# Up stages: the first pair's convolution, gating and block sums handed out in pieces between the products of the first two seven-product items

## The chip, the cores and the metric

The kernel runs on one core of a Trainium2 chip. The time is that of one execution in device microseconds (us). Four engines matter here: PE (TensorE, the matrix products), DVE (VectorE), ACT (ScalarE) and POOL (GpSimd); SP issues most of the transfers.

## The reference

A trunk of two layers on one sequence of S = 1024 rows, D = 1024 wide, in float32. Each layer has a mixer (layer 0 a gated delta rule, layer 1 retention) and a feed-forward part, each with a residual and a layer norm, scaled and shifted by vectors that come from a conditioning input through a product with an "adaptive" weight. The change touches the first half of the feed-forward part:

```python
def causal_dwconv(x, w):
    k_w = w.shape[0]
    s = x.shape[1]
    xp = jnp.pad(x, ((0, 0), (k_w - 1, 0), (0, 0)))
    y = xp[:, k_w - 1:k_w - 1 + s] * w[k_w - 1]
    for j in range(k_w - 1):
        y = y + xp[:, j:j + s] * w[j]
    return y

def conv_ffn(h, w_up, conv_w, conv_b, w_down):
    gate, up = jnp.split(h @ w_up, 2, axis=-1)
    gate = causal_dwconv(gate, conv_w) + conv_b
    return (jax.nn.silu(gate) * up) @ w_down
```

The hidden width is 2816, 22 tiles of 128, and the convolution has three taps along the sequence.

## The kernel before

**Numbers.** Every float32 operand of a product is split into a high part (an ACT copy, line 89) and a low part (a DVE subtraction, line 90); a product is three matmuls, lines 110 to 112 or, when it adds to a bank in use, line 1229. A matmul takes 128 x 128 weights and 512 columns.

**Up stage.** `layer_tail` runs the feed-forward part, once a layer. Its up product is cut into 22 items: 11 pairs of one gate item and one up item, each with 2 x 2 blocks (two tiles of the hidden width by two halves of the sequence). `strassen` runs them. The first two items (pair 0) are done plainly in four blocks: first the blocks that need the first half of the sequence (`side(n, 0)`, item 1 before item 0), whose results ACT copies out into `ahead` tiles (line 1256) because the second half of the normalized input is still being built (`build_T`, transposes at line 439, their copies at 441, sums over blocks at 464 to 470); then the rest (`side(n, 1)`). All items from 2 on go through `wino`, a Winograd scheme with seven products in place of eight. There `psub` (line 1279) makes sums of weight blocks on DVE, `block` splits each into a pair `wb`, and `prod` runs 12 matmuls on it.

**What a finished block does.** Each item has a sink, called with a result. A gate item's sink (line 1617 or 1619) puts it into `g`. After the fourth, `conv` does the three taps for the four blocks q = 0 to 3: ACT multiplies by the last tap (line 1628), DVE adds two taps (line 1633, two instructions a block), ACT applies the silu (line 1634). An up item's sink, `gated`, multiplies `o[q]` by the result (line 1647) and stores it; after the fourth, four sums and differences of the blocks (line 1654) make the operands of the down product's own seven-product scheme, and are stored too. In pair 0 these sums are on DVE, later on POOL.

**Order.** Each engine takes its instructions in one order, fixed when the program is built; a list scheduler sets it from the order of the code, so code that is written earlier tends to stand earlier. `bg_step` issues one unit of a background queue: products of the conditioning input with adaptive weights (`bg_ada`, lines 237 and 239 on DVE, for a row a matmul with ones at line 261 and an add at 262), and others. `wino` calls it twice an item. The first unit queued in an up stage is `bg_ada(i, 5, "row")`, the gain behind the feed-forward part. Layer 0's up stage is preceded by the output projection (`proj_ln`, lines 326 to 359) in two halves, with transposes for the first half (line 282) at the switch between them.

Of the kernel before, what the change touches and what calls it, by code (L numbers as in the profile page):

```python
# [12 lines left out]
ALU = mybir.AluOpType  # L13
# [20 lines left out]
def trunk_kernel(ctx: ExitStack, tc, A):  # L34
# [1188 lines left out]
    def strassen(hT0, xts, scale, shift, items, tags=("hTb", "hTb", "qkv", "qkv", "aux"), direct=False):  # L1223
# [23 lines left out]
        for n in (1, 0):  # L1247
# [6 lines left out]
            ahead[n] = [tl("cv", [P, 516], name="ah")[:, 0:HALF] for _ in range(2)]  # L1254
# [26 lines left out]

        def wino(n, sink):
            ua, ub = items[n][:2]
            wa, wb = tl("wr", [P, D]), tl("wr", [P, D])
# [15 lines left out]
            s4 = psub(a12, s2)  # L1300
            prod(s2, "T2", X)
            u2 = copy_of(X)
            s3 = psub(a11, a21)
            prod(s4, "22", Z)
            sink(1, Z, u2)
            bg_step()
            prod(s3, "T3", X)
            u3 = copy_of(X, "t2")
            sink(3, X, z5)
            sink(2, prod(a22, "T4"), u3)  # L1310
            bg_step()
# [4 lines left out]
        for n in range(2):  # L1316
            if not direct:
                sinks[n] = items[n][2]()
                for i in range(2):
                    sinks[n](2 * i, ahead[n][i], None)  # L1320
            X = side(n, 1)
            for i in range(2):
                sinks[n](2 * i + 1, X[i], None)
            if n == 0:
                rest()
            if items[n][3]:
                items[n][3]()
        for n in range(2, len(items)):
            wino(n, items[n][2]())
            if items[n][3]:  # L1330
# [252 lines left out]
    def layer_tail(i, mix, wout, xsrc, x_mid, x_out, ln_next, final):  # L1583
        sc2, sh2 = fold(i, 1, 2 * i)
        if i == 0:
            hT0 = []
# [6 lines left out]
            for h in hooks[KT:]:  # L1593
                h()
        else:
            mix.append((sc2, sh2))
            hT0, xts = proj_st(mix[0])
        bg_ada(i, 5, "row")
        bg_gain(2 * i, x_mid, xg[i + 1], "xT")
        if i == 0:  # L1600
            for j in (1, 0, 4, 3):
                bg_ada(1, j, "col")
        cw = vcol(f"ffn_conv{i}")
# [3 lines left out]

        def pair_items(fp):
            g, o = [], []
# [11 lines left out]

            def conv():
                for q in range(4):
                    f, hf = 2 * fp + q // 2, q % 2
                    gv = g[q // 2]
                    w = cw[:, 3 * f:3 * f + 3]
                    t = tl("qkv", [P, HALF], name="o")
                    act.activation(t, gv[:, hs(hf)], AF.Copy, scale=w[:, 2:3])  # L1628
                    for j in (1, 2):
                        c0 = HALF if hf else j  # L1630
                        c1 = HALF * (hf + 1)
                        tv = t[:, c0 - HALF * hf:]
# [390 lines left out]
```

## Time and profile before

| | |
|---|---|
| runs shown | 2936.68, 2944.91, 2948.51 us; median 2944.91 |
| the profiled execution | 2944.47 us, its span 2942.7 us |
| PE busy in the span | 2815.8 us, 13594 matmuls |
| DVE busy | 2208.4 us, 3976 instructions |
| ACT busy | 1314.9 us, 2413 instructions |
| POOL busy | 497.8 us, 517 instructions |
| mean granted TensorE clock | 0.983 |
| layer 0: last plain matmul of pair 0, first matmul of item 2 | 805.57, 810.65 us |
| layer 1: the same two | 2328.62, 2333.70 us |

Busy times overlap, since the engines run side by side. The span is from the first to the last instruction in the trace, and the execution's time has 1.77 us more around it. A time in a row of the trace counts from the span's start. In brackets behind a row stands how long the engine was idle before it, and which instruction ended that.

### The profile page before, as it was taken

Reading aid. Unit: us, or ns where it says so; the run is one execution under the profiler, and the core shown is the slowest. Engines: PE = TensorE matmul, PEld = TensorE weight load, DVE = VectorE, ACT = ScalarE, POOL = GpSimd, SP = SyncE. Lnnn points to the kernel's source line nnn. Section 1 sums busy time; section 2 is a strip of 40 time slices with the busy share of each in tenths; the row PEclk is TensorE's granted clock in tenths of the full one; section 3 lists DMA queues with packets and bytes.
Section 4 is the critical chain, followed back from the end, with each engine's and each line's share of the span. In section 5 each row is a group of like instructions: output and inputs, shape, how many; then the busy total and the mean of one; then the engine's idle time right before and its main releaser. Section 6 shows DMA issues by size and latency. Waiting matters only on the chain. (4 is left out here: it accounts for less than half of the span.)

```text
span 2942.7 us, 38900 instructions
## 1 busy us (share of the span) xinstructions
PE 2815.8 (96%) x13594; PEld 2298.3 (78%) x13594; DVE 2208.4 (75%) x3976; ACT 1314.9 (45%) x2413; POOL 497.8 (17%) x517
## 2 busy tenths in 40 slices
PE   8999899999999999999999999999999899999997
PEld 6887777887778888887778877777777788888886
DVE  6878788656688888868686665566689787777779
ACT  4745564444544444545333333222344544444543
POOL 0312221100013332200000021422202023331001
PEclk9999899999999999999999999999999999999999
DMA  7231222243255655755333364655663253334753
GB/s 279 80 119 62 80 79 80 83 167 137 93 176 175 208 189 188 270 185 184 132 136 115 129 231 145 208 171 170 194 231 131 102 165 133 135 126 162 291 184 115
DMA packets 248276, 459.01 MB, mean 156 GB/s; under 512 B 23632, under 2 KB 77264, under 8 KB 248080
## 3 DMA queue, kind: packets, MB, share of 16 engines
q1 hardware_dynamic: 215680, 404.87, 40.9%
q10 hardware_dynamic: 29760, 43.00, 4.0%
q0 software_dynamic: 2640, 8.65, 0.8%
q8 instruction: 107, 1.75, 0.2%
q14 instruction: 89, 0.73, 0.1%
HBM read 343.71 MB, written 112.72 MB: 155 GB/s over the span
## 5 line engine op out<-in xcount | busy, mean ns | idle before, releaser
L714 PE MATMUL acc<-hT,wh 128*128 128x512 f32 x960 | 301.3, 395 | 0.0
L1504 PE MATMUL acc<-bb,ab 128*128 128x512 f32 x984 | 236.2, 398 | 10.9 <-DVE bb L90 9.3
L1504 PEld LDWEIGHTS acc<-bb,ab 128*128 128x128 f32 x984 | 186.0, 191 | 55.2 <-DVE bb L90 14.2
L714 PEld LDWEIGHTS acc<-hT,wh 128*128 128x128 f32 x960 | 183.4, 191 | 34.5
L1229 PE MATMUL acc<-T,wb 128*128 128x512 f32 x840 | 203.6, 391 | 6.9 <-DVE wb L90 6.8
L89 ACT ACTIVATE ab<-ar 128x512 fp32r<-128x512 f32 x210 | 130.2, 626 | 171.2 <-PE mm L303 46.9
L714 PE MATMUL acc<-hT,wl 128*128 128x512 f32 x480 | 202.3, 421 | 0.0
L411 POOL TENSOR_TENSOR xg<-xg,gb 128x512 f32<-128x512 f32 x48 | 62.4, 1302 | 773.6 <-DMA xg<-xs 761.4
L1229 PEld LDWEIGHTS acc<-T,wb 128*128 128x128 f32 x840 | 156.5, 188 | 45.0 <-DVE wb L90 10.4
L90 DVE TENSOR_TENSOR ab<-ar,ab 128x512 fp32r<-128x512 f32 x210 | 147.5, 708 | 57.6 <-ACT ab L89 57.6
L90 DVE TENSOR_TENSOR wl<-wr,wh 128x1024 fp32r<-128x1024 f32 x98 | 123.0, 1256 | 86.9 <-ACT wh L89 86.7
L1654 POOL TENSOR_TENSOR o<-o 128x512 f32<-128x512 f32 x80 | 124.7, 1568 | 288.8 <-ACT pc L1290 190.1
L90 DVE TENSOR_TENSOR wb<-wr,wb 128x512 fp32r<-128x512 f32 x162 | 116.9, 726 | 71.6 <-ACT wb L89 69.4
L89 ACT ACTIVATE wh<-wr 128x1024 fp32r<-128x1024 f32 x98 | 103.9, 1062 | 143.5 <-PE acc L714 70.5
L90 DVE TENSOR_TENSOR wb<-mm,wb 128x512 fp32r<-128x512 f32 x216 | 145.8, 683 | 27.5 <-ACT wb L89 26.8
L1633 DVE SCALAR_TENSOR_TENSOR o<-g,vc,o 128x512 f32<-128x512 f32 (+2 forms) x176 | 155.0, 897 | 5.3 <-ACT o L1628 4.6
L89 ACT ACTIVATE wb<-mm 128x512 fp32r<-128x512 f32 x216 | 124.0, 595 | 64.4 <-DVE mm L1279 61.3
L1290 ACT ACTIVATE pc<-acc 128x512 f32<-128x512 f32 x143 | 84.6, 592 | 144.2 <-PE acc L1229 88.5
L89 ACT ACTIVATE wb<-wr 128x512 fp32r<-128x512 f32 x162 | 98.6, 627 | 107.6 <-DMA wr<-in_ffn_up 50.2
L714 PE MATMUL acc<-wh,hT 128*128 128x512 f32 x384 | 135.2, 416 | 1.0 <-DVE vv L90 1.0
L110 PE MATMUL acc<-T,wb 128*128 128x512 f32 x292 | 116.0, 397 | 9.4 <-DVE wb L90 9.4
L490 DVE SCALAR_TENSOR_TENSOR qkv<-raw,vc,qkv 128x512 f32<-128x512 f32 x144 | 110.3, 769 | 14.2 <-ACT qkv L488 13.5
(651 smaller groups left out, 7456.4 us busy)
## 6 DMA issues: line engine op xcount, KB each, us to landing
wr<-in_ffn_up SPq DMA_DIRECT2D x92, 512.0 KB, 4.3
mvw<-in_ada_w SPq DMA_DIRECT2D x80, 512.0 KB, 4.4
ad<-o SPq DMA_DIRECT2D x154, 256.0 KB, 3.1
ar<-ad SPq DMA_DIRECT2D x154, 256.0 KB, 3.8
Br<-in_ffn_down SPq DMA_DIRECT2D x88, 256.0 KB, 3.4
wr<-in_ret_wv SPq DMA_DIRECT2D x32, 512.0 KB, 4.2
ar<-od SPq DMA_DIRECT2D x56, 256.0 KB, 4.9
wr<-in_gdn_wqkv SPq DMA_DIRECT2D x24, 512.0 KB, 3.5
```

The costliest lines, as they stand in the source:

```text
L89: act.activation(dst_h, src, AF.Copy)
L90: eng.tensor_tensor(dst_l, src, dst_h, ALU.subtract)
L110: mm(acc, wl[:, k], hl[0], start=first, stop=False)
L411: pool.tensor_tensor(x, x, gb[0], ALU.mult)
L490: dve.scalar_tensor_tensor(oh, raw[:, 3 - j:515 - j], w[:, 3 - j:4 - j], oh, ALU.mult, ALU.add)
L714: pq(pe.matmul(out, lhsT, rhs, start=start, stop=stop), cost)
L1229: return pe.matmul(*a, skip_group_check=True, **kw)
L1290: act.activation(t, X, AF.Copy)
L1504: return pe.matmul(*args, skip_group_check=True, **kw)
L1633: dve.scalar_tensor_tensor(tv, gv[:, c0 - j:c1 - j], w[:, 2 - j:3 - j], tv, ALU.mult, ALU.add)
L1654: (dve if fp == 0 else pool).tensor_tensor(o[d], o[x], o[y], op)
```

## The change

Only `strassen` and `layer_tail` are touched, and of `strassen` only the calls from the two up stages take the new paths.

- A list `late` holds pieces of work. `drain(n)` takes up to n of them off its front and issues them. `wino` drains two behind s4's difference, two behind s3's, two behind the sink of block 1 and two behind the sink of block 3; behind every item from 3 on, all that is left.
- Pair 0's convolution goes into the list as four pieces, in the order q = 1, 3, 0, 2, where it ran at once for q = 0 to 3. Then come the gating of the two blocks just computed, the gating of the two `ahead` blocks, and the four block sums, one piece each. A gating piece first issues pieces until its own block's convolution has been issued. Pair 1's convolution goes through the list too.
- While the list holds work at an item's start, that item calls no `bg_step`. Layer 0's `bg_ada(0, 5, "row")` is queued ahead of the output projection, with its weights in "xT" tiles; layer 1's stays in the up stage, behind the gain.
- The two `ahead` copies of item 1 share one "xT" tile in place of two "cv" tiles.

The number of instructions on each engine is the same before and after; POOL's order is unchanged.

DVE at the entry of item 2 in layer 0, up to the low half of the first block `wb`, which the first product waits for. `T4` is the last low half of the input's sums, `o` the convolution's blocks and `g` a gate result of item 2; the scalar multiply-and-add of the convolution is printed as TENSOR_SCALAR. Before:

```order
L90 TENSOR_TENSOR T4_7372<-bt_7213,T4_7371 128x512
L1633 TENSOR_SCALAR o_7375<-g_7223,vc_144,o_7375 128x511
L1619 TENSOR_TENSOR g_7472<-sc_7501,pc_7494 128x512
L1633 TENSOR_SCALAR o_7380<-g_7223,vc_144,o_7380 128x512
L1633 TENSOR_SCALAR o_7375<-g_7223,vc_144,o_7375 128x510
L1633 TENSOR_SCALAR o_7385<-g_7224,vc_144,o_7385 128x511
L1633 TENSOR_SCALAR o_7390<-g_7224,vc_144,o_7390 128x512
L1633 TENSOR_SCALAR o_7380<-g_7223,vc_144,o_7380 128x512
L90 TENSOR_TENSOR wb_7517<-mm_7496,wb_7517 128x512
```

After, from the same low half of `T4`:

```order
L90 TENSOR_TENSOR T4_7415<-bt_7256,T4_7414 128x512
L1661 TENSOR_SCALAR o_7545<-g_7266,vc_144,o_7545 128x512
L1648 TENSOR_TENSOR g_7480<-sc_7509,pc_7502 128x512
L1661 TENSOR_SCALAR o_7550<-g_7267,vc_144,o_7550 128x512
L1661 TENSOR_SCALAR o_7545<-g_7266,vc_144,o_7545 128x512
L90 TENSOR_TENSOR wb_7525<-mm_7504,wb_7525 128x512
```

Of the eight convolution steps six stood between `T4` and `wb`, and three do now.

The next stretch of DVE there, up to the low half of the second product's block. `ada` is the adaptive row, `mm` a sum of weight blocks, `ah` and `acc` the up results that gate `o`. Before:

```order
L237 TENSOR_SCALAR ada_7609<-mvw_7572,e_154 128x512
L1633 TENSOR_SCALAR o_7385<-g_7224,vc_144,o_7385 128x510
L1647 TENSOR_TENSOR o_7375<-o_7375,ah_7071 128x512
L1633 TENSOR_SCALAR o_7390<-g_7224,vc_144,o_7390 128x512
L1279 TENSOR_TENSOR mm_7535<-wr_7474,mm_7515 128x512
L1647 TENSOR_TENSOR o_7380<-o_7380,acc_7405 128x512
L239 TENSOR_SCALAR ada_7609<-mvw_7572,e_154,ada_7609 128x512
L1647 TENSOR_TENSOR o_7385<-o_7385,ah_7072 128x512
L1647 TENSOR_TENSOR o_7390<-o_7390,acc_7436 128x512
L90 TENSOR_TENSOR wb_7537<-mm_7515,wb_7537 128x512
```

After:

```order
L1661 TENSOR_SCALAR o_7574<-g_7266,vc_144,o_7574 128x511
L1661 TENSOR_SCALAR o_7550<-g_7267,vc_144,o_7550 128x512
L1661 TENSOR_SCALAR o_7579<-g_7267,vc_144,o_7579 128x511
L1283 TENSOR_TENSOR mm_7543<-wr_7482,mm_7523 128x512
L1684 TENSOR_TENSOR o_7545<-o_7545,acc_7424 128x512
L1661 TENSOR_SCALAR o_7574<-g_7266,vc_144,o_7574 128x510
L1661 TENSOR_SCALAR o_7579<-g_7267,vc_144,o_7579 128x510
L1684 TENSOR_TENSOR o_7550<-o_7550,acc_7455 128x512
L90 TENSOR_TENSOR wb_7555<-mm_7523,wb_7555 128x512
```

The two adaptive steps and the gating by the `ah` tiles have left, and three convolution steps have come in from the stretch ahead.

ACT in layer 1, while the second half of the input is built. `bt` are transposed blocks, `12`, `22` and `T3` high halves of them. Before:

```order
L89 ACTIVATE 12_20075<-bt_20066 128x512
L89 ACTIVATE 22_20078<-bt_20073 128x512
L441 ACTIVATE bt_20086<-mm_20081,fh11_18758,fs11_18757 128x512
L441 ACTIVATE bt_20093<-mm_20088,fh11_18758,fs11_18757 128x512
L89 ACTIVATE 12_20095<-bt_20086 128x512
L89 ACTIVATE 22_20098<-bt_20093 128x512
```

After:

```order
L89 ACTIVATE 12_20073<-bt_20064 128x512
L89 ACTIVATE T3_20161<-bt_20031 128x512
L89 ACTIVATE 22_20076<-bt_20071 128x512
L441 ACTIVATE bt_20084<-mm_20079,fh11_18757,fs11_18756 128x512
L1260 ACTIVATE ah_19950<-acc_19894 128x512
L1260 ACTIVATE ah_19950<-acc_19925 128x512
L441 ACTIVATE bt_20091<-mm_20086,fh11_18757,fs11_18756 128x512
L89 ACTIVATE 12_20093<-bt_20084 128x512
L89 ACTIVATE 22_20096<-bt_20091 128x512
```

The high half `12` of the last tile has one more high half (`T3`) and the two `ah` copies of item 1 ahead of it; before, these three stood further up.

In layer 0 the two ones-matmuls of line 261 now stand in the output projection on PE, the first behind the 96th of its product matmuls, the second between the first half's last product matmul and the 24 transposes at the switch; the add of the second (line 262) is between two low halves on DVE there.

The diff:

```diff
--- before.py
+++ after.py
@@ -1220,7 +1220,7 @@
         dve.tensor_tensor(b, a, b, ALU.add)
         return b
 
-    def strassen(hT0, xts, scale, shift, items, tags=("hTb", "hTb", "qkv", "qkv", "aux"), direct=False):
+    def strassen(hT0, xts, scale, shift, items, tags=("hTb", "hTb", "qkv", "qkv", "aux"), direct=False, late=()):
         B = {"11": hT0[:4], "21": hT0[4:]}
         nblk = [0]
         nacc = [0]
@@ -1251,7 +1251,11 @@
                 for i in range(2):
                     sinks[n](2 * i, X[i], None)
                 continue
-            ahead[n] = [tl("cv", [P, 516], name="ah")[:, 0:HALF] for _ in range(2)]
+            if n:
+                t = tl("xT", [P, 2, HALF], name="ah")
+                ahead[n] = [t[:, 0], t[:, 1]]
+            else:
+                ahead[n] = [tl("cv", [P, 516], name="ah")[:, 0:HALF] for _ in range(2)]
             for t, x in zip(ahead[n], X):
                 act.activation(t, x, AF.Copy)
         rest = build_T(B, xts, scale, shift, tags)
@@ -1279,8 +1283,13 @@
             dve.tensor_tensor(t, x, y, op)
             return t
 
+        def drain(n):
+            for _ in range(min(n, len(late))):
+                late.pop(0)()
+
         def wino(n, sink):
             ua, ub = items[n][:2]
+            early = bool(late)
             wa, wb = tl("wr", [P, D]), tl("wr", [P, D])
             sp.dma_start(wa, ua)
             anchor["wi"] = sp.dma_start(wb, ub)
@@ -1298,17 +1307,23 @@
             Z = prod(s1, "T1")
             z5 = copy_of(Z)
             s4 = psub(a12, s2)
+            drain(2)
             prod(s2, "T2", X)
             u2 = copy_of(X)
             s3 = psub(a11, a21)
+            drain(2)
             prod(s4, "22", Z)
             sink(1, Z, u2)
-            bg_step()
+            if not early:
+                bg_step()
+            drain(2)
             prod(s3, "T3", X)
             u3 = copy_of(X, "t2")
             sink(3, X, z5)
+            drain(2)
             sink(2, prod(a22, "T4"), u3)
-            bg_step()
+            if not early:
+                bg_step()
             if n > 4:
                 row_step()
 
@@ -1316,17 +1331,25 @@
         for n in range(2):
             if not direct:
                 sinks[n] = items[n][2]()
-                for i in range(2):
-                    sinks[n](2 * i, ahead[n][i], None)
+                if n == 0:
+                    for i in range(2):
+                        sinks[n](2 * i, ahead[n][i], None)
             X = side(n, 1)
             for i in range(2):
-                sinks[n](2 * i + 1, X[i], None)
+                if direct or n == 0:
+                    sinks[n](2 * i + 1, X[i], None)
+                else:
+                    late.append(lambda i=i, x=X[i]: sinks[1](2 * i + 1, x, None))
             if n == 0:
                 rest()
             if items[n][3]:
                 items[n][3]()
+        if not direct:
+            late += [lambda i=i: sinks[1](2 * i, ahead[1][i], None) for i in range(2)]
         for n in range(2, len(items)):
             wino(n, items[n][2]())
+            if n > 2:
+                drain(len(late))
             if items[n][3]:
                 items[n][3]()
         bg_tag[0] = "wr"
@@ -1583,6 +1606,8 @@
     def layer_tail(i, mix, wout, xsrc, x_mid, x_out, ln_next, final):
         sc2, sh2 = fold(i, 1, 2 * i)
         if i == 0:
+            bg_ada(0, 5, "row")
+            bg_tag[0] = "xT"
             hT0 = []
             get = out_hl(mix)
             G1 = rows[0, 2]
@@ -1592,21 +1617,25 @@
             hooks = ln_hooks(1, xts, "hTa", lambda: (sc2, sh2), [], x_mid, ("mid", i))
             for h in hooks[KT:]:
                 h()
+            bg_tag[0] = "wr"
         else:
             mix.append((sc2, sh2))
             hT0, xts = proj_st(mix[0])
-        bg_ada(i, 5, "row")
         bg_gain(2 * i, x_mid, xg[i + 1], "xT")
         if i == 0:
             for j in (1, 0, 4, 3):
                 bg_ada(1, j, "col")
+        else:
+            bg_ada(1, 5, "row")
         cw = vcol(f"ffn_conv{i}")
         cb = vcol(f"ffn_convb{i}")
         ad = dr.tile([NF // 2, 7, P, HALF], F32, tag=f"ad{i}", name=f"ad{i}")
         up = A["ffn_up"][i]
 
+        late = []
+
         def pair_items(fp):
-            g, o = [], []
+            g, o = [], {}
 
             def gate_start():
                 g.extend(tl("lane", [P, D], name="g") for _ in range(2))
@@ -1619,20 +1648,26 @@
                         dve.tensor_tensor(dst, a, b, ALU.add)
                 return gate
 
+            def conv_q(q):
+                f, hf = 2 * fp + q // 2, q % 2
+                gv = g[q // 2]
+                w = cw[:, 3 * f:3 * f + 3]
+                t = tl("qkv", [P, HALF], name="o")
+                act.activation(t, gv[:, hs(hf)], AF.Copy, scale=w[:, 2:3])
+                for j in (1, 2):
+                    c0 = HALF if hf else j
+                    c1 = HALF * (hf + 1)
+                    tv = t[:, c0 - HALF * hf:]
+                    dve.scalar_tensor_tensor(tv, gv[:, c0 - j:c1 - j], w[:, 2 - j:3 - j], tv, ALU.mult, ALU.add)
+                act.activation(t, t, AF.Silu, bias=cb[:, f:f + 1])
+                o[q] = t
+
             def conv():
-                for q in range(4):
-                    f, hf = 2 * fp + q // 2, q % 2
-                    gv = g[q // 2]
-                    w = cw[:, 3 * f:3 * f + 3]
-                    t = tl("qkv", [P, HALF], name="o")
-                    act.activation(t, gv[:, hs(hf)], AF.Copy, scale=w[:, 2:3])
-                    for j in (1, 2):
-                        c0 = HALF if hf else j
-                        c1 = HALF * (hf + 1)
-                        tv = t[:, c0 - HALF * hf:]
-                        dve.scalar_tensor_tensor(tv, gv[:, c0 - j:c1 - j], w[:, 2 - j:3 - j], tv, ALU.mult, ALU.add)
-                    act.activation(t, t, AF.Silu, bias=cb[:, f:f + 1])
-                    o.append(t)
+                for q in (1, 3, 0, 2) if fp == 0 else range(4):
+                    if fp < 2:
+                        late.append(lambda q=q: conv_q(q))
+                    else:
+                        conv_q(q)
 
             def store(nm, q):
                 sp.dma_start(ad[fp, ABLK.index(nm)], o[q])
@@ -1641,6 +1676,8 @@
                 seen = []
 
                 def gated(q, a, b):
+                    while q not in o:
+                        late.pop(0)()
                     c = a
                     if b is not None:
                         dve.tensor_tensor(c, a, b, ALU.add)
@@ -1651,13 +1688,18 @@
                     if len(seen) == 4:
                         for d, x, y, op, nm in ((1, 1, 3, ALU.add, "S1"), (0, 1, 0, ALU.subtract, "S2"),
                                                 (2, 2, 0, ALU.subtract, "S4"), (3, 3, 0, ALU.subtract, "S3")):
-                            (dve if fp == 0 else pool).tensor_tensor(o[d], o[x], o[y], op)
-                            store(nm, d)
+                            def one(d=d, x=x, y=y, op=op, nm=nm):
+                                (dve if fp == 0 else pool).tensor_tensor(o[d], o[x], o[y], op)
+                                store(nm, d)
+                            if fp == 0:
+                                late.append(one)
+                            else:
+                                one()
                 return gated
 
             return [(up[4 * fp], up[4 * fp + 2], gate_start, conv), (up[4 * fp + 1], up[4 * fp + 3], up_start, None)]
 
-        strassen(hT0, xts, sc2, sh2, [it for fp in range(NF // 2) for it in pair_items(fp)])
+        strassen(hT0, xts, sc2, sh2, [it for fp in range(NF // 2) for it in pair_items(fp)], late=late)
         while rowq or rowp:
             row_step()
         slots = {"c": "hTa", "x": "qkv"}
```

## The prediction

> **What bounds the kernel now.** I read the busy table first, then the clock line of the slices, then the waits, and last the rows where PE waits.
>
> ```profile
> PE 2815.8 (96%) x13594; PEld 2298.3 (78%) x13594; DVE 2208.4 (75%) x3976; ACT 1314.9 (45%) x2413; POOL 497.8 (17%) x517
> PEclk9999899999999999999999999999999999999999
> ```
>
> PE is busy for 2815.8 of 2942.7 us, so this is a PE kernel: an edit pays only where it takes away a PE wait or a run at a lower clock, and 127 us of the span is all that PE does not fill. The waits of 740 to 900 us, around the first up stage, name two that the change can reach (columns: us in total, times, longest):
>
> ```profile
> PE acc L110 <- DVE wb L90: 4.7, 1, 4.7
> PE acc L1229 <- DVE wb L90: 0.5, 1, 0.5
> ```
>
> They stand at the entry of the first seven-product item. PE and DVE there in order of time (start, duration):
>
> ```profile
> 805.57 0.39 PE L112 MATMUL sc<-hT,wb 128*128 128x512 f32 x1
> 810.65 0.80 PE L110 MATMUL acc<-T,wb 128*128 128x512 f32 x1 [4.69 <-DVE wb L90]
> 815.51 0.63 PE L112 MATMUL acc<-T,wb 128*128 128x512 f32 x1
> 816.63 3.03 PE L1229 MATMUL acc<-T,wb 128*128 128x512 f32 x12 [0.49 <-DVE wb L90]
> ```
>
> ```profile
> 806.00 0.69 DVE L1619 TENSOR_TENSOR g<-sc,pc 128x512 f32<-128x512 f32 x1 [0.22 <-PE sc L112]
> 806.61 3.39 DVE L1633 SCALAR_TENSOR_TENSOR o<-g,vc,o 128x512 f32<-128x512 f32 x5
> 809.91 0.68 DVE L90 TENSOR_TENSOR wb<-mm,wb 128x512 fp32r<-128x512 f32 x1
> 810.51 0.48 DVE L237 TENSOR_SCALAR ada<-mvw,e 128x512 f32<-128x512 f32 x1
> 810.91 0.74 DVE L1633 SCALAR_TENSOR_TENSOR o<-g,vc,o 128x510 f32<-128x510 f32 x1
> ...
> 815.89 1.28 DVE L90 TENSOR_TENSOR wb<-mm,wb 128x512 fp32r<-128x512 f32 x2
> ```
>
> PE has nothing after 805.57 until DVE has written the low half of s1's block (809.91 + 0.68 = 810.59), 0.06 before PE's 810.65. In front of that low half stand five convolution steps in a row. The second low half lands at 815.89 + 0.68 = 816.57, and PE follows at 816.63, 0.06 later again. From 805.57 to 816.63 PE runs 13 matmuls, which at the rate of the second product (12 in about 2.7 us, 0.227 each) are worth 2.95 us: **8.1 us are lost at this entry.** The first product's matmuls stand 0.427 apart, because the clock is halved; by windows (columns: length, busy us of PE, PEld, DVE, ACT, POOL with counts, granted clock, DMA):
>
> ```profile
> 805.82:809.23 3.41, 0.14 (x1) 0.00 (x0) 3.23 (x5) 2.21 (x4) 0.00 (x0) 1.00 0.00 0
> 809.23:812.64 3.41, 1.99 (x5) 1.60 (x6) 3.41 (x7) 1.45 (x2) 0.00 (x0) 0.50 0.00 0
> 812.64:816.06 3.42, 3.42 (x9) 2.20 (x7) 3.42 (x7) 1.69 (x3) 0.00 (x0) 0.50 0.20 77
> 816.06:819.47 3.41, 2.92 (x13) 2.36 (x13) 3.41 (x6) 1.72 (x3) 0.00 (x0) 1.00 0.63 234
> ```
>
> The second layer's entry is the same picture, 1523.05 us later:
>
> ```profile
> 2328.62 0.39 PE L112 MATMUL sc<-hT,wb 128*128 128x512 f32 x1
> 2333.70 0.80 PE L110 MATMUL acc<-T,wb 128*128 128x512 f32 x1 [4.69 <-DVE wb L90]
> 2339.68 2.54 PE L1229 MATMUL acc<-T,wb 128*128 128x512 f32 x10 [0.79 <-DVE wb L90]
> ```
>
> **The change, part by part.** No instruction is added or removed on any engine; all is order.
>
> **A, DVE at the entry.** The steps on DVE, by start to start: a convolution step 0.66 (3.30 for the five from 806.61), an add or low half 0.60 (809.91 to 810.51). Three convolution steps are still ahead of the first low half, one of them ahead of the gate sum at 806.00. So two follow the gate sum where five do: 806.61 + 2 x 0.66 = 807.93, low half done at 808.61, PE at 808.67 instead of 810.65: **1.98 earlier**. Then, up to the second product's low half, the order after has three convolution steps, a difference, a gating product, two convolution steps and a gating product: 807.93 + 0.60 + 5 x 0.66 + 3 x 0.60 = 813.63, done 814.31, PE at 814.37 instead of 816.63: **2.26 earlier**. The first product is not on that path: started at 808.67, its 12 matmuls end by 811.4 at full rate and by 813.8 at half rate, both ahead of 814.37. What goes in one wait comes back partly in the other: the first shrinks from 4.85 to 2.87 us, the second grows to 0.6 at half rate or 3.0 at full rate. The gating and the block sums that now stand behind these rows have cover, but it is thin: the third low half stands directly behind the second (done at 814.9), and of the fourth I find 819.2, counted on in the same way, against 819.8, when PE asks for it (814.37 and two products of 12 x 0.227). From there a delay would come through one for one; I keep it at nothing, and so 2.26. The other layer's DVE rows lie the same way: 2 x 2.26 = **-4.52**. ACT's high halves are not late:
>
> ```profile
> 804.28 2.55 ACT L1628 ACTIVATE o<-g,vc 128x512 f32<-128x512 f32 x4
> 806.73 0.58 ACT L89 ACTIVATE wb<-mm 128x512 fp32r<-128x512 f32 x1
> ```
>
> The first one was done at 807.31 behind four convolution starts; with two ahead of it, it is some 1.2 us sooner, before 807.93.
>
> **B, clock.** What PE's idle time costs at a threshold is shown nearest by another place:
>
> ```profile
> 1372.44:1375.85 3.41, 1.35 (x7) 0.78 (x6) 2.63 (x5) 3.09 (x7) 0.00 (x0) 1.00 1.01 404
> 1375.85:1379.26 3.41, 3.41 (x10) 2.67 (x9) 3.41 (x7) 1.68 (x5) 0.00 (x0) 0.50 0.77 278
> ```
>
> Idle 2.06 of 3.41 us in one window, and the next window runs at half clock. In A the window from 805.82 would still be idle for 2.7 us, so the first product meets half clock again, hidden behind DVE: cost 0. If the windows lie otherwise, the gate can close in the second wait and slow products that nothing hides: 8 matmuls x 0.20 (0.427 less 0.227) in one window, 16 in two, so 0 to +3.2 a layer. I take 0, by the row of this very place. The Trainium skill ("TensorE: Matmul & The Clock Gate", section "What's actually happening") states a free-running window of 4096 cycles, about 3.4 us, with the gate shut after a whole idle window; the length agrees with the 3.41 here. By its "at least one idle window" neither wait (2.87, 3.0) could shut the gate, and the second rival below would have no chance; the row with 2.06 us idle speaks against that, so the measurement decides and the rival stays.
>
> **C, the adaptive row (layer 0 only).** Its two ones-matmuls leave the up stage, where they cost PE time in full:
>
> ```profile
> 856.22 1.52 PE L1229 MATMUL acc<-T,wb 128*128 128x512 f32 x6
> 857.58 1.02 PE L261 MATMUL mm<-ada,ones 128*128 128x512 f32 x2
> 858.03 1.26 PE L1229 MATMUL sc<-22_7158,wb 128*128 128x512 f32 x3
> 859.12 0.85 PE L1229 MATMUL sc<-22_7178,wb 128*128 128x512 f32 x3
> ```
>
> From 857.58 to 859.12 are 1.54 us, of which three product matmuls are 0.68: 0.86 each, -1.72. They reappear in the output projection, one between product matmuls in a full PE (+0.86), the other ahead of the transposes at the half switch:
>
> ```profile
> 714.55 1.03 PE L282 MATMUL mm<-cst,xt 128*128 128x128 f32 x8
> 716.53 1.32 PE L282 MATMUL mm<-cst,xt 128*128 128x128 f32 x8 [0.94 <-ACT t L284]
> ...
> 722.73 0.80 PE L326 MATMUL acc<-wh,hl 128*128 128x512 f32 x1 [1.86 <-DVE t L356]
> ```
>
> That stretch is a chain of transposes, ACT and DVE, so a late start passes through: +0.86, with 0 as its lower end (hidden in these waits) and 0.86 + 0.69 as its upper end (the sum L262 on DVE, an add of 0.69, in line as well). Sum **0**, bounds -0.9 to +0.7; with the first hidden too, -1.7. The row's 16 multiply steps on DVE, at 0.40 to 0.66 some 5 us for each half, go along, into these two stretches:
>
> ```profile
> 564.30:579.50 15.20, 15.20 (x204) 12.94 (x204) 4.05 (x6) 3.32 (x5) 0.00 (x0) 0.80 0.18 66
> 667.00:714.50 47.50, 47.50 (x216) 39.29 (x215) 31.46 (x54) 20.77 (x26) 2.15 (x4) 1.00 0.44 155
> ```
>
> DVE is idle there for 11 and 16 us while PE is never idle, so they cost nothing, and the eight loads that SP issues for them meet DMA engines at 0.18 and 0.44; without that cover each step would be 0.66. In the up stage the steps that left (one stood at 810.51) are in A already.
>
> **D, layer 1's copies.** The two copies of item 1's first side move, on ACT, behind the transposes' copies and ahead of the fourth tile's high half, with one more split:
>
> ```profile
> 2291.56 0.60 ACT L1256 ACTIVATE ah<-acc 128x512 f32<-128x512 f32 x1 [2.42 <-PE acc L112]
> 2297.82 1.46 ACT L441 ACTIVATE bt<-mm,fh,fs 128x512 f32<-128x512 f32 x2
> 2299.14 0.66 ACT L89 ACTIVATE 12_20095<-bt 128x512 fp32r<-128x512 f32 x1
> ```
>
> ```profile
> 2301.25 0.50 PE L111 MATMUL acc<-12_20095,wh 128*128 128x512 f32 x1 [0.45 <-DVE 12_20095 L90]
> ...
> 2310.91 0.50 PE L110 MATMUL acc<-12_20035,wl 128*128 128x512 f32 x1 [0.40 <-DVE wl L90]
> ```
>
> Two copies at about 0.49 (2291.56 to the next start) and a split at 0.52 make the high half up to 1.5 late, done 2301.3; DVE's low half adds 0.68 and PE the 0.06: 2302.05, against 2301.25: +0.8. The lower end is 0 (DVE and PE wait 0.92 and 0.40 further on and may absorb it), the upper 1.5. I take **+0.8**.
>
> **Sum:** -4.52 + 0 + 0 + 0.8 = -3.7. The profiled execution took 2944.47 us (span 2942.7 and 1.77 around it), 0.4 under the runs' median of 2944.91: **2940.8 us**.
>
> **Rivals.** **R1, the whole entry loss goes:** first wait, half clock and second wait all vanish, 8.1 a layer: 2944.47 - 16.2 + 0.8 = 2929.1. For it: the convolution work is meant to lie between products, and it is over 6 us of DVE. Against it: three convolution steps remain ahead of the first low half and eight rows between the two. **R2, slower:** with the first product ending early, at full rate, the second wait is 3.0 us and shuts the gate there. It decides when more than about 2 us of idle fall into one 3.41 window that ends in the second product. With two windows at half clock, 3.2 - 2.26 = +0.94 a layer: 2944.47 + 1.9 + 0.8 = 2947.2; with one, 2944.0. Against it: in the rows above the first window is idle enough to halve the first product, and then the second wait is short. **R3, nothing happens at the entry:** a low half elsewhere in the queue, or an ACT copy, is the true limit and the change does not do what it says: 2944.47 + 0.8 = 2945.3. Against it: PE followed the low halves by 0.06 at both products.
>
> **Numbers.** Forecast 0.65, R1 0.08, R2 0.17, R3 0.10. The known bounds run from -4.52 - 1.7 = 2938.3 to -4.52 + 6.4 + 0.7 + 1.5 = 2948.6. Against the profiled 2944.47, runs of before went from 2936.68 to 2948.51, so a median can stand some us off either end: **2931 to 2950**, which leaves out part of R1. A measurement of this kernel tells about 0.5% (14.7 us) from no change. R1 alone gets there, just, and half of it counts: faster 0.07, with some for what I have not seen; slower needs +14.7, which no case gives: 0.04. **Faster 0.09, same 0.87, slower 0.04.**
>
> **What would show it.** The first low half at about 2.0 us less behind the gate sum, the PE wait there at 2.7 and not 4.69, and the second product 8.8 us behind the last gate-side matmul instead of 11.06 in both layers: A. Half clock in the first product and none in the second: B. The ones-matmul gone from 857 and a later first projection matmul by 0 to 1.5 after the half switch: C. PE's matmul of the fourth tile 0.8 later: D. It is wrong if second-product matmuls stand 0.427 apart, or if PE waits elsewhere for low halves that the moved gating pushed back.

## The result, and the profile after

The changed kernel takes **2939.07 us** (median of 22 runs, 2934.91 to 2944.72), the kernel before 2943.84 us (22 runs, 2936.11 to 2953.45): ratio 0.9984, 95% interval 0.9977 to 0.9992, so 4.7 us less (2.4 to 6.8). The forecast was 2940.8 us, 3.7 less. The profiled execution took 2940.32 us, its span 2938.6 us. Its busy table and clock line:

```profile
PE 2810.8 (96%) x13594; PEld 2291.5 (78%) x13594; DVE 2210.9 (75%) x3976; ACT 1316.6 (45%) x2413; POOL 500.1 (17%) x517
PEclk9999999999999999999999999999999999999999
```

Still a PE kernel, and counts are as before. The entry of item 2 in layer 0, PE in order of time, then DVE:

```profile
806.21 0.39 PE L112 MATMUL sc<-hT,wb 128*128 128x512 f32 x1
809.31 0.79 PE L110 MATMUL acc<-T,wb 128*128 128x512 f32 x1 [2.71 <-DVE wb L90]
...
813.36 0.40 PE L112 MATMUL acc<-T,wb 128*128 128x512 f32 x1
815.00 3.03 PE L1229 MATMUL acc<-T,wb 128*128 128x512 f32 x12 [1.25 <-DVE wb L90]
```

```profile
806.64 0.69 DVE L1648 TENSOR_TENSOR g<-sc,pc 128x512 f32<-128x512 f32 x1 [0.22 <-PE sc L112]
807.24 1.41 DVE L1661 SCALAR_TENSOR_TENSOR o<-g,vc,o 128x512 f32<-128x512 f32 x2
808.57 0.68 DVE L90 TENSOR_TENSOR wb<-mm,wb 128x512 fp32r<-128x512 f32 x1
809.17 2.06 DVE L1661 SCALAR_TENSOR_TENSOR o<-g,vc,o 128x511 f32<-128x511 f32 x3
...
814.27 1.28 DVE L90 TENSOR_TENSOR wb<-mm,wb 128x512 fp32r<-128x512 f32 x2
```

Two convolution steps follow the gate sum where five did, and PE follows each low half by 0.06 us as before. What the prediction calls the first and second product are the third and fourth of the item's seven, those of s1 and s2; the two ahead of them run without a wait. From the last matmul ahead of the wait, s1 starts 3.10 us later (before 5.08) and s2 8.79 (before 11.06). Layer 1's entry is the same to 0.01:

```profile
2325.24 0.39 PE L112 MATMUL sc<-hT,wb 128*128 128x512 f32 x1
2328.34 0.79 PE L110 MATMUL acc<-T,wb 128*128 128x512 f32 x1 [2.71 <-DVE wb L90]
...
2334.03 3.04 PE L1229 MATMUL acc<-T,wb 128*128 128x512 f32 x12 [1.30 <-DVE wb L90]
```

The clock in layer 0's entry, by windows (columns as in the prediction):

```profile
805.57:808.98 3.41, 1.03 (x5) 0.53 (x3) 3.19 (x6) 2.67 (x6) 0.00 (x0) 1.00 0.00 0
808.98:812.39 3.41, 3.08 (x7) 2.48 (x8) 3.41 (x7) 1.67 (x4) 0.00 (x0) 0.50 0.00 0
812.39:815.80 3.41, 2.17 (x9) 1.43 (x8) 3.41 (x7) 2.96 (x6) 0.00 (x0) 1.00 0.17 67
```

One window at half clock where there were two, inside s1's product, and s2 waits for DVE behind it all the same.

A new wait is in item 5, 23 products behind s1's at seven an item (the expectations below call it item 4). DVE stands still for adaptive weights, with a convolution queued behind them. It is pair 2's, which runs at once; only pairs 0 and 1 go through the list. In layer 1:

```profile
2387.81 0.75 DVE L239 SCALAR_TENSOR_TENSOR ada<-mvw,e,ada 128x512 f32<-128x512 f32 x1 [2.78 <-DMA mvw<-in_ada_w]
2388.48 0.74 DVE L1661 SCALAR_TENSOR_TENSOR o<-g,vc,o 128x511 f32<-128x511 f32 x1
```

```profile
2395.03 0.96 PE L1229 MATMUL acc<-22_20036,wb 128*128 128x512 f32 x3 [0.76 <-ACT pc L1299]
```

The late convolution makes ACT's silu late (it ends at 2394.49), the copy `pc` stands behind the silu on ACT, and PE waits for the bank that the copy frees: 0.92 us beyond the usual distance, and 0.60 in layer 0, where DVE waits 1.16.

To see how far one trace can be trusted, the changed kernel, the kernel before and that of e1 (below) were traced a second time. Lengths in us between matmuls' starts: from the trace's start to the first of the output projection, from that to the last ahead of the entry, from that to s2, and from s2 to the last matmul of line 1229 in the up stage:

| | to the projection | projection to entry | entry 0 | rest of up stage 0 | entry 1 | rest of up stage 1 |
|---|---|---|---|---|---|---|
| before | 642.19 | 163.38 | 11.06 | 382.29 | 11.06 | 375.05 |
| before, again | 635.67 | 164.29 | 11.05 | 383.82 | 11.06 | 376.69 |
| changed | 642.24 | 163.97 | 8.79 | 380.62 | 8.79 | 377.06 |
| changed, again | 637.90 | 165.65 | 8.79 | 382.35 | 8.79 | 376.84 |
| e1 | 637.97 | 163.82 | 4.62 | 382.87 | 4.63 | 376.97 |
| e1, again | 638.39 | 164.22 | 4.62 | 381.43 | 4.62 | 378.77 |

The entry repeats to 0.01 us. The stages differ by 0.2 to 1.8 us between two executions of one kernel, and the start by up to 6.5, so a difference of 1 us in a stage, read from one trace each, is no finding.

> The changed kernel once more, for a second trace of it. If what the up stages give back behind the entry belongs to the kernel, the rest of layer 0's up stage, from s2 on, is 380.6 us again and that of layer 1 377.1, each to 0.5, with the waits of 0.60 and 0.92 us in item 4; if it belongs to the single execution, these lengths differ by 1 us or more and the waits lie elsewhere.

> The kernel before once more, for a second trace of it. If the stages' lengths belong to the kernel: 382.3 us from s2 to the end of layer 0's up stage, 375.0 in layer 1, each to 0.5. If to the single execution: 1 us or more apart. The entry stays at 11.06 us in either case.

> The kernel of e1 once more, for a second trace. If the stages' lengths belong to the kernel: entry 4.62 us, then 382.9 us to the end of layer 0's up stage and 377.0 in layer 1, each to 0.5; if to the single execution, 1 us or more apart, the entry as it was.

The answer is in the table: entries belong to the kernel, the lengths of the stages behind only to 1 or 2 us. The item-5 wait of layer 1 does belong to the kernel (0.90 in the second trace), that of layer 0 only in part (0.33). The three single times were 2941.92, 2949.21 and 2930.75 us.

### The profile page after: what moved, and what is told of

The parts are those of the page before. It is cut to its first block, busy times and chain, and to the rows that moved or that the text cites. A ratio compares the mean times of both kernels' runs of the same rounds, so it can differ in the third digit from the quotient of the medians.

```text
span 2938.6 us, 38910 instructions
## 1 busy us (share of the span) xinstructions
PE 2810.8 (96%) x13594; PEld 2291.5 (78%) x13594; DVE 2210.9 (75%) x3976; ACT 1316.6 (45%) x2413; POOL 500.1 (17%) x517
## 5 line engine op out<-in xcount | busy, mean ns | idle before, releaser
L1527 PE MATMUL acc<-bb,ab 128*128 128x512 f32 x984 | 232.9, 394 | 11.6 <-DVE bb L90 10.2
L490 DVE SCALAR_TENSOR_TENSOR qkv<-raw,vc,qkv 128x512 f32<-128x512 f32 x144 | 111.6, 778 | 14.7 <-ACT qkv L488 13.8
```

The source lines that it names most:

```text
L490: dve.scalar_tensor_tensor(oh, raw[:, 3 - j:515 - j], w[:, 3 - j:4 - j], oh, ALU.mult, ALU.add)
L1527: return pe.matmul(*args, skip_group_check=True, **kw)
```

## The experiments

The theory: the gain is the order of DVE at the entry, twice 2.27 us. Rivals: the moved row brings it (its two DVE steps stood in the entry), or the new order of the convolution's blocks does.

**e1: all low halves first.** The changed kernel, with the list's pieces queued on DVE behind the low half of the block last split, and the first two pairs handed out one product later:

```diff
 def block(src):
-    split(t[:, 0], t[:, 1], src)
+    anchor["lo"] = split(t[:, 0], t[:, 1], src)   # returns the DVE instruction
 def drain(n):
-        late.pop(0)()
+        with after("lo"):
+            late.pop(0)()
 s4 = psub(a12, s2)
-drain(2)
 prod(s2, "T2", X)
+drain(2)
 u2 = copy_of(X)
 s3 = psub(a11, a21)
-drain(2)
 prod(s4, "22", Z)
+drain(2)
```

> The changed kernel, with every piece of the list queued on DVE behind the low half of the block last split, and the first two pairs of pieces handed out one product later, so that at the entry of item 2 no convolution step stands ahead of the low halves of s1 and s2. Theory (DVE's order is what is left of the entry loss): from the last matmul ahead of the wait to the first of s2's product 4.5 us, against 8.79 in the changed kernel and 11.06 before, in both layers: s1 starts about 1.8 us after that matmul, s2 with no wait. That is 4.3 less a layer, 8.6 in all, 2930.5 us, if nothing comes back. Rival 1: the convolution and gating that now lie later hold the two banks of the plain up results or delay the low halves of items 2 and 3, and PE waits there instead: entry 4.5 us, time 2936 to 2942. Rival 2: ACT's high halves or the gate sum are the limit, not DVE's order: the wait at s1 stays above 2.5 us, time 2939.

2932.93 us (5 runs, 2928.72 to 2937.08), ratio to before 0.9957 (0.9944 to 0.9970): 12.7 us less, and the lowest median of all versions. PE and DVE at its entry:

```profile
801.79 0.39 PE L112 MATMUL sc<-hT,wb 128*128 128x512 f32 x1
803.56 0.50 PE L110 MATMUL acc<-T,wb 128*128 128x512 f32 x1 [1.38 <-DVE wb L90]
...
806.41 2.88 PE L1229 MATMUL acc<-T,wb 128*128 128x512 f32 x12
...
813.34 2.83 PE L1229 MATMUL acc<-T,wb 128*128 128x512 f32 x11 [1.33 <-DVE wb L90]
```

```profile
802.22 0.69 DVE L1649 TENSOR_TENSOR g<-sc,pc 128x512 f32<-128x512 f32 x1 [0.89 <-PE sc L112]
802.82 0.68 DVE L90 TENSOR_TENSOR wb<-mm,wb 128x512 fp32r<-128x512 f32 x1
803.54 0.69 DVE L1283 TENSOR_TENSOR mm<-wr,mm 128x512 f32<-128x512 f32 x1
804.90 0.69 DVE L90 TENSOR_TENSOR wb<-mm,wb 128x512 fp32r<-128x512 f32 x1 [0.67 <-ACT wb L89]
805.51 1.41 DVE L1662 SCALAR_TENSOR_TENSOR o<-g,vc,o 128x512 f32<-128x512 f32 x2
```

No convolution step stands ahead of s1 or s2, s2 follows s1 without a wait, and no window at half clock is left there. The entry is 4.62, as the theory had it (4.5), 6.44 less than before. Part of that comes back in one wait of 1.33 us ahead of s3's product, whose low half is now behind the convolution: counted to the start of s3's product, e1 stands at 11.55 and 11.56 us, the changed kernel at 14.37 and 14.39, before at 16.65 and 16.61. That is 5.1 us a layer, 10.2 in all, inside the 8.8 to 16.5 by which the time fell; which part of the other 2.5 us is real, two traces can't tell. The loss at the entry is the order on DVE.

**e2 and e3: the row alone, both ways.** e2 is the changed kernel with layer 0's row back in the up stage, e3 the kernel before with only the row moved:

```diff
 # e2, in layer_tail of the changed kernel
 if i == 0:
-    bg_ada(0, 5, "row")
-    bg_tag[0] = "xT"
...
-    bg_tag[0] = "wr"
...
+if i == 0:
+    bg_ada(0, 5, "row")
 bg_gain(2 * i, x_mid, xg[i + 1], "xT")
```

> The changed kernel, with layer 0's adaptive row queued in the up stage again, ahead of the gain, as before (items 2 and 3 still call no background step). Theory (the gain at the entry comes from the order of convolution and gating, the row's move is a term of its own worth about 1.1): entry 8.79 us as in the changed kernel, the time from the first matmul of the output projection to the entry back at 163.4 (changed: 163.97), two ones-matmuls in layer 0's up stage again for 1.7: 2940.2 us. Rival (the row's move is what brings the gain, since its DVE steps stood in the entry): entry above 10 us in layer 0, 2943 us or more.

2962.76 us (6 runs), ratio 1.0059 (1.0046 to 1.0072): **17.4 us slower than before**, though its entries are 8.79 us in both layers. So the row's move does not bring the entry's gain, but neither side foresaw what its absence costs. The loss is in layer 0's down product, 246.43 us long where it is 224.83 in the changed kernel (from the last matmul of line 1229 ahead of it to its own last). Its worst wait:

```profile
1218.28 0.80 PE L301 MATMUL acc<-bb,ab 128*128 128x512 f32 x1 [10.75 <-DVE ab L90]
```

DVE still has adaptive steps among the down product's first low halves there:

```profile
1207.98 0.48 DVE L237 TENSOR_SCALAR ada<-mvw,e 128x512 f32<-128x512 f32 x1
1208.38 0.68 DVE L1683 TENSOR_TENSOR o<-o,sc 128x512 f32<-128x512 f32 x1
1208.98 2.83 DVE L90 TENSOR_TENSOR ab<-ar,ab 128x512 fp32r<-128x512 f32 x2
1211.74 0.74 DVE L239 SCALAR_TENSOR_TENSOR ada<-mvw,e,ada 128x512 f32<-128x512 f32 x1
```

The count explains why they are there: five vectors of 8 units are 40 units, and 20 items of two steps are 40 steps. Items 2 and 3 now skip four steps, so four units spill into the down product. Without the row the queue holds 32 units for 36 steps. How four units make a wait of 10.75 us is not shown: the steps of DVE in these rows are far shorter, and the low half that ends the wait (1217.54) stands behind a high half that ACT could start only at 1217.02, having stood 2.32 us for the load of its block.

```diff
 # e3, in layer_tail of the kernel before
 if i == 0:
+    bg_ada(0, 5, "row")
+    bg_tag[0] = "xT"
...
+    bg_tag[0] = "wr"
...
-bg_ada(i, 5, "row")
+if i:
+    bg_ada(i, 5, "row")
```

> The kernel before, with only layer 0's adaptive row moved ahead of the output projection. Theory: 11.06 us at layer 1's entry, and at layer 0's 11.06 less the two adaptive steps that stood between the two low halves, 0.40 and 0.66, so about 10.0; the projection 0.6 longer and two ones-matmuls of 0.86 gone from the up stage: 1.1 and 1.1 less, 2941.6 us. As the prediction's term C had it (0 net): 2942.8. Rival (the row's move brings the whole gain): 2939 to 2940.

2941.81 us (12 runs), ratio 0.9986 (0.9974 to 0.9997), 4.1 less (0.9 to 7.7): as large as the gain of the whole change, so by its time alone the rival would stand. Its entry shows that it is another gain:

```profile
809.74 0.80 PE L110 MATMUL acc<-T,wb 128*128 128x512 f32 x1 [4.69 <-DVE wb L90]
815.71 0.98 PE L1229 MATMUL acc<-T,wb 128*128 128x512 f32 x3 [0.76 <-DVE wb L90]
```

With 804.66 as the last matmul ahead, that is 5.08 and 11.05. My 10.0 was wrong: the next vector of the queue takes the row's place in items 2 and 3, and its steps stand at the same point on DVE.

**e9: nothing handed out.** The changed kernel with each piece issued where it is queued, and the background steps kept:

```diff
+class Now(list):        # append and += call the piece at once
-late = []
+late = Now()
```

> The changed kernel, with every piece issued at the place where it is queued, so that nothing is handed out between products; the new order of the convolution's blocks, the moved row and the xT tile stay, and items 2 and 3 call their background steps. Theory (handing out is what frees the entry, the order of the blocks alone does nothing): six convolution steps ahead of s1's low half again, entry 11.06 us in both layers; the time is that of the row's move alone, 2941 to 2943. Rival (the order of the blocks is what matters): entry 10 us or less, 2940.

2944.82 us (12 runs), ratio 0.9995 (0.9981 to 1.0009). The entry is 5.08 and 11.66 in both layers:

```profile
812.48 0.79 PE L110 MATMUL acc<-T,wb 128*128 128x512 f32 x1 [4.69 <-DVE wb L90]
819.06 1.20 PE L1229 MATMUL acc<-T,wb 128*128 128x512 f32 x4 [1.48 <-DVE wb L90]
```

The new order of blocks, the moved row and the shared tile gain nothing at the entry without the handing out; s2 is even 0.6 later, one DVE step more (a block sum ahead of its low half). With e3 it leaves the row's own worth between nothing and some us.

**e5: background steps kept in items 2 and 3.**

```diff
-early = bool(late)
+early = False
```

> The changed kernel, with the background steps of items 2 and 3 called as in the kernel before. Theory (the new waits of PE in item 4, 0.60 us in layer 0 and 0.92 in layer 1, come from the pause: the first adaptive weights after it are loaded late, DVE waits 1.16 and 2.78 us for them with the convolution behind): these two waits go, and the two adaptive steps (0.40 and 0.66) stand between the two low halves of the entry again: s2 at 9.85 us after the last matmul, not 8.79. Sum about +2.1 - 1.5 - up to 1.5 for smaller waits behind: 2938 to 2940. Rival (the waits in item 4 come from pair 1's convolution pieces): waits stay, entry 9.85: 2941.

2945.57 us (12 runs), ratio 1.0000 (0.9988 to 1.0013). Its entry is 9.85 in both layers, as worked out, and PE's wait for the copy in item 5 is gone from both: it comes from the pause. But the time is more than 5 us above what was expected. Its trace shows where most of that goes, just behind the entry. PE at s2, then the clock by windows, in layer 0:

```profile
811.68 4.52 PE L1229 MATMUL acc<-T,wb 128*128 128x512 f32 x12 [2.28 <-DVE wb L90]
```

```profile
808.09:811.50 3.41, 1.30 (x6) 0.75 (x4) 3.41 (x6) 3.19 (x6) 0.00 (x0) 1.00 0.08 32
811.50:814.91 3.41, 3.23 (x8) 2.56 (x9) 3.41 (x7) 0.03 (x1) 0.00 (x0) 0.50 0.49 182
```

With the two adaptive steps back, the second wait is 2.28 us (2.41 in layer 1), the clock halves behind it in both layers, and s2's product takes 4.36 and 4.23 us where it takes 2.86 and 2.87 in the changed kernel. This is the prediction's R2. Counted to the start of s4's product, e5 stands at 14.21 and 14.08 us, the changed kernel at 11.65 and 11.67, before at 13.93 and 13.89: all that the handing out gains there is gone. Against the changed kernel that is 5.0 us for both layers, less up to 1.5 for the waits in item 5, where the ratios are 4.7 us apart. This is one trace, of an execution of 2940.18 us, 5 under e5's median, so the sum fits the medians without proving them; but the pause is a condition of the gain at the entry.

**e4: layer 1's row early as well.** The changed kernel with layer 1's row ahead of its output projection:

```diff
 mix.append((sc2, sh2))
+bg_ada(1, 5, "row")
+bg_tag[0] = "xT"
 hT0, xts = proj_st(mix[0])
+bg_tag[0] = "wr"
...
-else:
-    bg_ada(1, 5, "row")
```

> The changed kernel, with layer 1's adaptive row moved as layer 0's was: queued ahead of layer 1's output projection, weights in xT tiles, none of it in the up stage. Theory (what layer 1's up stage gave back, 2.0 us, comes from the row's late weights: DVE waits 2.78 us for them in item 4, the convolution behind them and the ACT copy that PE waits for 0.92 us are late): the 0.92 us wait is gone, the two ones-matmuls cost the up stage nothing (1.7), and the up stage from its entry to its last product is 3 to 4 us shorter than 385.85; some of the ones-matmuls' 1.7 comes back in the projection: 2935.5 to 2937.5. Rival (the wait comes from the convolution pieces of pair 1): the wait stays, up stage shorter by 1.7 at most, projection longer by as much: 2939.

2949.61 us (9 runs), ratio 1.0020 (1.0010 to 1.0030), 5.9 **slower** than before. The theory of the item-5 wait holds: it is gone from layer 1, and up stage 1 is 382.89 us long in place of 385.85, 3.0 less. But from the last matmul of the retention's own seven-product items to the entry (the retention, its output projection and the plain items), 574.23 us became 587.84 (577.07 in the changed kernel's second trace). PE's waits from 2186 us to the entry, in e4 and in the changed kernel:

```profile
PE acc L1527 <- DVE bb L90: 8.0, 6, 2.1
PE acc L110 <- DVE wl L90: 4.7, 2, 3.7
```

```profile
PE acc L1527 <- DVE bb L90: 3.0, 6, 1.2
PE acc L110 <- DVE wl L90: 0.8, 1, 0.8
```

PE waits for DVE's low halves there already, and with the row's steps on DVE it waits longer: 8.9 us longer in these two rows, of 13.6. Where the rest lies was not traced further. The move that was harmless in layer 0 is dear in layer 1.

**e6 and e7: the low halves before everything.** e6 is e1 with the pieces starting behind s4's low half (four at once) and item 2's first gate sum behind s1's; e7 is e6 with the background steps kept, queued behind the last low half too:

```diff
-sink(0, prod(a12, "21"), p1)
+Y = prod(a12, "21")
+if not early:
+    sink(0, Y, p1)
 s2 = psub(s1, a11)
 Z = prod(s1, "T1")
+if early:
+    with after("lo"):
+        sink(0, Y, p1)
...
 prod(s2, "T2", X)
-drain(2)
...
 prod(s4, "22", Z)
-drain(2)
+drain(4)
...
-if not early:                                  # e7 alone
+with after("lo") if early else nullcontext():
     bg_step()
```

> As e1, and the pieces start one product later still, behind the low half of s4's block, and item 2's first gate sum stands behind s1's low half. Theory: s1 starts 0.6 earlier than in e1 (1.2 us after the last matmul, not 1.77), s2 at 4.0 instead of 4.6, the 1.49 us wait of s4's product in e1 goes: 2 us less a layer than e1, 2929, if the later pieces find room. Rival: the pieces crowd into item 3 and come back there as waits for its low halves (e1 shows such waits of 0.91 and 1.12 already): no better than e1, 2932 to 2934.

> As e6, and the background steps of items 2 and 3 are called, their DVE steps queued behind the low half of the block last split. Theory: entry as in e6 (s2 at 4.0), and the waits of item 4 that the pause brought (0.67 and 0.65 in e1) are gone: 1 to 3 us below e6, 2926 to 2928. Rival (DVE is full in items 2 and 3, so two more units there come back as waits for low halves): 2930 or more.

e6 took 2933.64 us (7 runs), ratio 0.9964 (0.9951 to 0.9978): no better than e1, as the rival had it. The entry is 4.15, but the wait that I had placed at s4 belongs to s3, which is still behind the convolution, and it grew to 1.79 us: s3's product starts 11.54 us after the last matmul ahead, in e1 11.55. In layer 0 the wait halves the clock behind it as well:

```profile
811.46:814.87 3.41, 1.61 (x8) 1.26 (x8) 3.41 (x6) 3.14 (x5) 0.00 (x0) 1.00 0.75 257
814.87:818.28 3.41, 3.41 (x10) 2.67 (x9) 3.27 (x7) 0.61 (x2) 0.00 (x0) 0.50 0.41 159
```

e7 took 2941.12 us (12 runs), ratio 0.9991 (0.9978 to 1.0003). The entry is 4.15 again, and layer 0's up stage 397.65 us long, longer than before the change (393.35): behind the wait at s3 (2.20 us) lie nine more for low halves, each 0.46 us or more beyond the usual distance of two matmuls. The three largest, of 1.09 to 1.90 us, come 45 to 71 us behind the last matmul ahead of the entry. That the pieces and the background units crowd DVE there fits, but no run separates the two.

**e8: the copies in two cv tiles again.**

```diff
-if n:
-    t = tl("xT", [P, 2, HALF], name="ah")
-    ahead[n] = [t[:, 0], t[:, 1]]
-else:
-    ahead[n] = [tl("cv", [P, 516], name="ah")[:, 0:HALF] for _ in range(2)]
+ahead[n] = [tl("cv", [P, 516], name="ah")[:, 0:HALF] for _ in range(2)]
```

> The changed kernel, with the two copies of item 1 in two cv tiles again, as before. Theory (term D: in layer 1 the copies wait on ACT for the xT tile and delay the fourth tile's high half): the stage from the end of the down product before it to the entry is back at 60.75 us (changed 61.14), 0.4 less, 2938.7 us. Rival (the cv tiles are the shorter supply: two stay taken until the ahead blocks are gated, and the copies of products in item 2 wait for one): PE waits for a bank or a copy in item 2, 1 to 3 us a layer, 2941 to 2945.

2943.02 us (11 runs), ratio 0.9996 (0.9987 to 1.0004). By its rows the theory holds and the rival does not. From the first matmul of layer 1's plain items to the last one ahead of the entry it is 60.12 us, as before (60.14, and 60.09 in the second trace), where the changed kernel has 60.45 and 60.47; no wait for a bank or copy stands in item 2. Counted from the last product matmul of the output projection, as the expectation meant it, it is 60.86, with 61.14 and 61.32 in the changed kernel and 60.75 and 61.12 before: a wait of PE ahead of the plain items, which differs from execution to execution, hides the third of a microsecond. By its time the kernel is no faster than the changed one (0.9977 to 0.9992); whether it is slower, the overlapping intervals don't tell.

## Why the prediction was right, point by point

**A was right to 0.01 us in both layers**: 3.10 and 8.80 forecast, 3.10 and 8.79 measured, and the low halves decided it (e1, e9). Its second wait was neither 0.6 nor 3.0 but 1.25, since the half clock lasted one window. The thin cover held: from s2 on PE shows no wait in items 2 and 3. What gave way was item 5, and by another road: A looked at the next low halves, not at the pause of the background queue and the late weights behind it. That is up to 1.5 us for both layers, which the sum left out.

**B was right**: half clock hidden, 0. **R2**, the gate shutting in an unhidden wait, did not come in the changed kernel, and keeping it as a rival was right: e5 is its case, with 2.11 us idle in one window (3.41 less 1.30) and about 1.4 us lost a layer, and e6 shows it from 1.80 us idle. What kept it away is that the changed kernel's second wait is 1.25 and not 2.28 us, for which the two skipped adaptive steps are enough; term A counted them as gone, without saying that B hangs on them. The Trainium skill ("TensorE: Matmul & The Clock Gate", section "What's actually happening") asks for a whole idle window of about 3.4 us. The rows of e5 and e6 disagree with that, as the one quoted in the prediction did.

**C was mis-sized.** The half switch, PE in the changed kernel:

```profile
716.02 1.02 PE L261 MATMUL mm<-ada,ones 128*128 128x512 f32 x2
716.87 0.60 PE L282 MATMUL mm<-cst,xt 128*128 128x128 f32 x4
717.82 1.18 PE L282 MATMUL mm<-cst,xt 128*128 128x128 f32 x8 [0.35 <-DVE rowb L262]
...
724.10 0.80 PE L326 MATMUL acc<-wh,hl 128*128 128x512 f32 x1 [1.91 <-DVE t L356]
```

From the last matmul ahead (715.79) to the next half's first are 8.31 us, before 8.41 (714.32 to 722.73): the matmul that I priced at 0.86 is hidden. By rows C is -1.72 + 0.86 - 0.10, about -1.0 in place of 0, just outside its bounds of -0.9 to +0.7. e3 alone measured 0.9 to 7.7 less. I also took the row for a term of its own; e2 shows it to be a condition of the change, worth 22 us (1.0059 less 0.9984) once the steps are skipped.

**D was too large.** 0.8 was forecast, with 0 and 1.5 as its ends. The fourth tile's matmul, of which the prediction shows the row before, is later by more than that:

```profile
2299.25 0.39 PE L111 MATMUL acc<-12_20093,wh 128*128 128x512 f32 x1
```

From the first matmul of the plain items (2268.48 before, 2264.79 after) to the line-111 matmul it was 32.77 us and is 34.46, so 1.69 later. But the waits behind take up most of it, as the prediction allowed for: to the last matmul ahead of the entry it is 60.45 and 60.47 us against 60.14 and 60.09, 0.35 more. In e8, with the two tiles of before, it is 60.12. The other traces agree: 60.16 in e3, 60.43 to 60.48 in the kernels with the shared tile (only e4, with its row's steps there, has 61.91). So this small term is real, and it is under half of the forecast.

**The sum**: -4.54, -1.0, +0.35 and up to +1.5 for item 5 make -3.7, where -4.7 (2.4 to 6.8 less) was measured. That interval does not reach zero, though the prediction put the least that can be told at 14.7 us. That this is the forecast's own -3.7 is luck: the errors of C (1.0) and D (0.45) cancel the missing wait (1.5). A and D are shown by runs that undo them; C's -1.0 is read from rows alone.

**R1** had the size of the loss right (8.1 a layer; e1 got 6.44 back at s2, 5.1 counted to s3) and its reason against was the true one: the order left three convolution steps ahead of one low half and eight rows ahead of the other. **R3** is ruled out by the 0.06 us.

## What to carry to other kernels

An engine that feeds the bound one is a queue: count what stands ahead of the one instruction that is waited for, by start-to-start times, and the gain at that place follows to a hundredth (8.80 forecast, 8.79 measured). Count on past it, too: a wait there can halve the clock and undo the gain, as in e5, or move to the next product, as in e1 and e6. Code written later is not issued later if a scheduler finds it ready: the pieces are written behind s1's product, and three of their steps still stand ahead of its low half. e1 tied the filler behind the waited-for instruction and got nearly three times the gain. Whoever skips turns of a background queue must count turns against units, since the rest spills into the next stage.

## What the runs showed of the hardware

The granted clock fell to 0.50 for a window of 3.41 us after windows in which PE was idle 1.80 us (e6), 2.11 us (e5) and 2.38 us (changed kernel). It stayed at 1.00 over e1's wait of 1.38 us at the entry, and over e6's wait of 1.80 us at s3 in layer 1, so the length of a wait alone does not decide it. After the entry's 4.69 us half clock took two windows in layer 0 of both traces of before; in layer 1 it took two in one trace and one in the other. Two executions of one kernel differ by up to 6.5 us in their first 640 us, and by 0.2 to 1.8 us in an up stage, while the entry, which hangs on DVE's order, repeats to 0.01.
